# A gated attention layer on one core: the last attention unit's z and gate fill in pieces behind the logits of its second to sixth group, and the second gate weight split behind the sixth group's rows

## The chip, the core and the metric

The kernel runs on one core of a Trainium2 chip. The core has five engines with a queue of instructions each, worked off in order: TensorE (PE in the profile, its weight loads PEld), VectorE (DVE), ScalarE (ACT), GpSimd (POOL) and SyncE (SP), which here only issues transfers. Engines wait for each other by semaphores. TensorE writes into PSUM, which is divided into banks; the kernel keeps small pools of them. The metric is the time of one execution in microseconds (us), as the median of several runs.

## What is computed

One decoder layer for 1024 positions of 1024 channels, in float32. From the normed input one projection makes queries, keys, values, forget logits, z (the SiLU gates of the branches) and two gates per channel. Two attention branches follow: eight "fox" heads of 64 channels with a forget bias, and four "diff" heads with two maps each.

```python
h = rms_norm(x, g_pre[l], NORM_EPS)
proj = jnp.einsum('bsd,dn->bsn', h, w_in[l])
qa, ka, va, fa, za, qb, kb, vb, zb, gates = jnp.split(proj, SPLIT_POINTS, axis=-1)
ya = fox_attention(...)            # logits + c_t - c_s, causal softmax, times v
ya = merge_heads(ya) * jax.nn.silu(za)
yb = diff_attention(qd, kd, vd, lam)
yb = merge_heads(rms_norm(yb, g_subln[l], SUBLN_EPS) * (1.0 - lam_init)) * jax.nn.silu(zb)
gate_a, gate_b = jnp.split(jax.nn.sigmoid(gates), N_BRANCHES, axis=-1)
merged = gate_a * (ya @ w_branch[l, 0]) + gate_b * (yb @ w_branch[l, 1])
x = x + rms_norm(merged @ w_out[l], g_post[l], NORM_EPS)
```

## The kernel before

Every large product is made of three float32r products, high times high, high times low and low times high part; so each operand is split: a high part (a cast, mostly on ScalarE) and a low part (a subtraction, mostly on VectorE). A projection of 128 channels and 512 positions (`project`) is 24 matmuls of 512 columns: eight slices `k` of the 1024 input channels, three products each.

**Stages.** First the normed and transposed input `hT` and the values (lines to 297). Then eight attention units `u`: 0 to 3 are diff heads, 4 to 7 pairs of fox heads. Then the gates (first `pg`, a plain projection, then products by Winograd's scheme, `x_g`), the branch products `pb`, and the output product `x_o`.

**A fox unit** has eight groups: four pairs of query blocks `g` (in the last units in the order 3, 2, 1, 0), for each head `m` of the two. A group has two rows `i` (blocks of 128 queries). `s_row` makes a row: one or two pairs of matmuls put logits `Sf` into a PSUM bank (L487, L488; a pool of three banks); VectorE adds the bias `cb` and takes the minimum in one reduction (L490: writes `Pf`, `mxf`); ScalarE takes the exponential (L496, sum `lf`); VectorE the reciprocal (L617); GpSimd scales (L618). Ahead of each row GpSimd adds the mask to the diagonal of `cb` (L613). The `Pf` rows lie in a pool of six buffers, so a row's reduction waits until the transposes of the row six before it have been read. Then the group's `products` (`av`): TensorE transposes four blocks of 128 into a bank `ptf` (L517, two banks), ScalarE makes the high part `phf` (L520), VectorE the low part `plf` (L521), TensorE multiplies with the values (L541, `ypf`, one bank), and ScalarE and VectorE move the result out of that bank (`yt` L627, `ys` L628). The products of a group are issued after the rows of the next one.

**Fill.** Between the groups stand projections that attention does not wait for: queries and keys of the next unit, and `z` of a slice (`spill_tasks`: matmuls into a bank `pz`, a copy L428, a store L429). In unit 7 the fill list is z6 and z7, two halves of 24 matmuls each. `gate = spill_tasks("gl", ...)` makes the first gate's slice 0 the same way in two halves: `gate[0]` behind the logits of the sixth group (`GFILL = 5`), `gate[1]` in pieces among the last products, where an order is written out by `then` (`issue_after(lasts[0])`: what is issued inside is not placed before that instruction). The second gate's slice 0 is `gates_plain(0)`: `load_w` loads the weight and splits it, high part `hi_g` on ScalarE (L315), low part `lo_g` on GpSimd (L319); its matmuls `pg` come after the attention.

**What sets the order.** The program is recorded as it is written, and a scheduler with a model of times of its own (`schedule_with_timeline_sim=True`) then places each engine's instructions. So the matmuls of z stand where that scheduler put them, between other rows; only `issue_after` holds them back. Buffers of the weights are in pools of two (`wraw`, `whi`, `wlo`): `hi_g` takes the buffer of an earlier high part, and the load of the next gates' weight (`gate_raw`, `raw_1`) the buffer that `lo_g` has read.

Of the kernel before, what the change touches and what calls it, by code (L numbers as in the profile page):

```python
# [11 lines left out]
AF = mybir.ActivationFunctionType  # L12
# [19 lines left out]
YORD = ((), ((4, 0), (4, 1)), ((5, 0), (5, 1), (6, 0)), ((6, 1), (7, 0), (7, 1)),  # L32
        ((0, 0), (0, 1), (1, 0)), ((1, 1), (2, 0), (2, 1)), ((3, 0), (3, 1)), ())
GFILL = 5
TAIL = 3
ZFILL = ((0,), (1,), (), (2,), (3,), (4,), (5,), (6, 7))
BIG = 3.0e38
# [12 lines left out]
def tile_hybrid_block(  # L50
# [254 lines left out]
                h_combinations(k)  # L305


    def load_w(name, src, hi_act=False, lo_pool=False, pieces=None):
        raw = wpool.tile([P, KT, P], F32, tag="wraw", name=f"raw_{name}")
        for ks, piece in pieces or [(slice(0, KT), src)]:  # L310
            nc.sync.dma_start(raw[:, ks], piece)
        hi = wpool.tile([P, KT, P], F32R, tag="whi", name=f"hi_{name}")
        lo = wpool.tile([P, KT, P], F32R, tag="wlo", name=f"lo_{name}")
        if hi_act:
            nc.scalar.copy(hi, raw)  # L315
        else:
            nc.gpsimd.tensor_scalar(hi, raw, 1.0, 1.0, op0=ALU.mult, op1=ALU.mult)
        eng = nc.gpsimd if lo_pool else nc.vector
        eng.tensor_tensor(lo, raw, hi, op=ALU.subtract)  # L319
        return hi, lo  # L320

    def w_cols(c0):
# [12 lines left out]
    with ExitStack() as st:  # L335
# [140 lines left out]
        def s_row(T, m, i, X, bias, boff, nm, le=None):  # L476

            A, B = (T["TA"], T["KA"]) if m == 0 else (T["TB"], T["KB"])
            n = (i + 1) * P
            qs = slice(i * P, (i + 1) * P)  # L480
            xs = slice(i % 2 * P, (i % 2 + 1) * P)
            pr = pp.tile([P, S], F32, tag="P", name=f"P{nm}_{m}_{i}")
            mx = small.tile([P, 2], F32, tag="mx", name=f"mx{nm}_{m}_{i}", bufs=8)
            pcs = pieces(i)
            for j, (a, b) in enumerate(pcs):
                ps = sps.tile([P, CH], F32, tag="S", name=f"S{nm}_{m}_{i}_{j}")[:, 0:b - a]
                nc.tensor.matmul(ps, lhsT=A[:, qs], rhs=B[:, a:b], start=True, stop=False)  # L487
                lasts[0] = nc.tensor.matmul(  # L488
                    ps, lhsT=X[:, xs], rhs=B[:, a:b], start=False, stop=True).ins
                nc.vector.tensor_tensor_reduce(  # L490
                    out=pr[:, a:b], in0=ps, in1=bias[:, boff + a:boff + b], scale=-0.125,
                    scalar=BIG if j == 0 else mx[:, j - 1:j], op0=ALU.add, op1=ALU.min,
                    accum_out=mx[:, j:j + 1])
            if le is None:
                le = small.tile([P, 1], F32, tag="l", name=f"l{nm}_{m}_{i}", bufs=8)
            nc.scalar.activation(pr[:, 0:n], pr[:, 0:n], AF.Exp,  # L496
                                 bias=mx[:, len(pcs) - 1:len(pcs)], scale=-1.0, accum_out=le)
            return pr, le

        def av(rows, g, vt, hoff, fox, evac, nm, final):  # L500
# [55 lines left out]
        def unit_attn(u, T):  # L556
# [19 lines left out]
            if diff:  # L576
                def row(i, rows):
                    boff = S - (i + 1) * P
                    if "X" not in rows:
                        rows["X"] = [swapped(T, m, i // 2, f"d{u}") for m in range(2)]  # L580
                    le = small.tile([P, 2], F32, tag="l2", name=f"l{u}_{i}", bufs=4)
                    l1, l2 = le[:, 0:1], le[:, 1:2]
                    p1, _ = s_row(T, 0, i, rows["X"][0], dmask, boff, f"d{u}", l1)
                    p2, _ = s_row(T, 1, i, rows["X"][1], dmask, boff, f"d{u}", l2)
                    n = (i + 1) * P
                    nc.vector.reciprocal(le, le)
                    nc.gpsimd.tensor_scalar(
                        p2[:, 0:n], p2[:, 0:n], l2, nlam, op0=ALU.mult, op1=ALU.mult)
                    nc.scalar.activation(p1[:, 0:n], p1[:, 0:n], AF.Copy, scale=l1)
                    nc.gpsimd.tensor_tensor(  # L590
                        p1[:, 0:n], p1[:, 0:n], p2[:, 0:n], op=ALU.add)
                    rows[i] = p1

                def evac(g):
                    def run(yp):
                        ys = stg.tile([P, 2 * P], F32, tag="ys", name=f"ys{u}_{g}")
                        nc.scalar.copy(ys, yp)
                        nc.sync.dma_start(y_d[u][:, g * 2 * P:(g + 1) * 2 * P], ys)
                    return run

                for g in GORD[u]:
                    rows = {}
                    groups.append((
                        4 * g + 3,
                        [lambda i=i, rows=rows: row(i, rows) for i in (2 * g, 2 * g + 1)],
                        lambda g=g, rows=rows: av(rows, g, vt, 0, False, evac(g), f"d{u}_{g}", False)))
            else:
                ysb = {}

                def row(m, i, rows):  # L610
                    n = (i + 1) * P
                    diag = cb[m][:, n - P:n]
                    nc.gpsimd.tensor_tensor(diag, diag, trim, op=ALU.add)  # L613
                    if "X" not in rows:
                        rows["X"] = swapped(T, m, i // 2, f"f{u}")
                    p1, l1 = s_row(T, m, i, rows["X"], cb[m], 0, f"f{u}")
                    nc.vector.reciprocal(l1, l1)  # L617
                    nc.gpsimd.tensor_scalar(  # L618
                        p1[:, 0:n], p1[:, 0:n], l1, 1.0, op0=ALU.mult, op1=ALU.mult)
                    rows[i] = p1  # L620

                def evac(m, g):
                    def run(yp):
                        if m == 0:
                            ysb[g] = stg.tile([P, 2 * P], F32, tag="ys", name=f"ys{u}_{g}")
                        tmp = stg.tile([P, 2 * P], F32, tag="yt", name=f"yt{u}_{m}_{g}", bufs=1)
                        nc.scalar.copy(tmp[64:128], yp[64:128])  # L627
                        nc.vector.tensor_tensor(  # L628
                            ysb[g][64 * m:64 * m + 64], yp[0:64], tmp[64:128], op=ALU.add)
                        if m == 1:  # L630
                            nc.sync.dma_start(y_d[u][:, g * 2 * P:(g + 1) * 2 * P], ysb[g])
                    return run

                for g in GORD[u]:
                    for m in range(2):
                        rows = {}
                        groups.append((
                            4 * g + 3,
                            [lambda m=m, i=i, rows=rows: row(m, i, rows) for i in (2 * g + 1, 2 * g)],
                            lambda m=m, g=g, rows=rows: av(  # L640
                                rows, g, vt, m * P, True, evac(m, g), f"f{u}_{m}_{g}",
                                u == 7 and g in FING)))
# [40 lines left out]
        for u in range(8):  # L683
# [13 lines left out]
            for t in SFILL[u]:  # L697
                fill += [lambda t=t, c=c: sum_squares(t, c) for c in range(2)]
                fill.append(lambda t=t: subln_scales(t))
            total = sum(s[0] for s in groups)  # L700
            done, nf = 0, 0
            for n, (wgt, rws, prd) in enumerate(groups):
                if n == len(groups) // 2 and u < 7:
                    nxt = unit_attn(u + 1, T)
                    vload.append(nxt[1])
                for r in rws:
                    r()
                if pend and (u < 7 or n <= TAIL):
                    products(*pend())
                if u == 7 and n >= TAIL:  # L710
                    tail.append(prd)
                pend = prd
                done += wgt
                while nf < len(fill) and nf < len(fill) * done / total:
                    fill[nf]()
                    nf += 1
                if u == 7 and n == GFILL:
                    with tc.issue_after(lasts[0]):
                        gate[0]()
                    break  # L720

        def then(*fns):
            for f in fns:
# [152 lines left out]

    def gates_plain(d):
        for br in (1,):
            wt = load_w(f"g{br}_{d}", w_cols(GT + br * D + d * P), True, True)
            yield  # L880
            for c in range(2):
                ps = xps.tile([P, CH], F32, tag="x", name=f"pg{d}_{br}_{c}")
                project(ps, wt, c)
                gate_out(d, br, c, tmp.tile([P, CH], F32, tag="t", name=f"g{d}_{br}_{c}"), ps)
# [287 lines left out]
```

## Time and profile before

| | us |
|---|---|
| median of 3 runs | 903.33 |
| lowest, highest | 903.07, 904.46 |
| the profiled execution | 901.91 |
| its span, from the first instruction to the last | 900.1 |
| granted TensorE clock, mean | 0.998 |
| stage of the last unit's groups | about 530 to 583 |

The profile is of one execution. Its page gives busy time by engine, the chain of waits that ended last, and groups of instructions; the trace answers with windows, waits and rows in order of time. Instructions go by tile names without buffer numbers, out<-in. The unit's number is not in them: `Sf` and `ptf` near 530 are of unit 6 and 7. A matmul's row shows a modelled end that reaches into the next one; the distance between starts tells more.

| stretch of the trace | PE busy | DVE busy | ACT busy | POOL busy |
|---|---|---|---|---|
| 500 to 520 | 19.70 | 10.61 | 13.43 | 11.18 |
| 520 to 540 | 20.00 | 9.01 | 7.67 | 4.13 |
| 540 to 560 | 17.98 | 16.87 | 15.49 | 13.89 |
| 560 to 580 | 19.66 | 11.69 | 12.11 | 6.40 |
| 580 to 600 | 20.00 | 7.91 | 8.92 | 8.45 |

### The profile page before, as it was taken

Reading aid. Unit: us, or ns where it says so; the run is one execution under the profiler, and the core shown is the slowest. Engines: PE = TensorE matmul, PEld = TensorE weight load, DVE = VectorE, ACT = ScalarE, POOL = GpSimd, SP = SyncE. Lnnn points to the kernel's source line nnn. Section 1 sums busy time; section 2 is a strip of 40 time slices with the busy share of each in tenths; the row PEclk is TensorE's granted clock in tenths of the full one; section 3 lists DMA queues with packets and bytes.
Section 4 is the critical chain, followed back from the end, with each engine's and each line's share of the span. In section 5 each row is a group of like instructions: output and inputs, shape, how many; then the busy total and the mean of one; then the engine's idle time right before and its main releaser. Section 6 shows DMA issues by size and latency. Waiting matters only on the chain.

```text
span 900.1 us, 13797 instructions
## 1 busy us (share of the span) xinstructions
PE 883.0 (98%) x4600; PEld 745.7 (83%) x4600; DVE 577.5 (64%) x1122; ACT 428.8 (48%) x865; POOL 403.8 (45%) x398
## 2 busy tenths in 40 slices
PE   8999999999999999999999999999999999999996
PEld 6999987788888888888888887888888888888885
DVE  6766555767666644456547548525686896648796
ACT  7523224665756653464645537624453362314352
POOL 2134224735647535254444526415534223483961
PEclk9999999999999999999999999999999999999999
DMA  9566656756557763645636432197766598210495
GB/s 303 190 239 250 219 164 164 176 136 171 155 137 191 180 170 84 180 103 128 190 92 170 130 88 60 61 410 242 244 198 207 189 344 304 79 39 1 122 197 172
DMA packets 138185, 154.79 MB, mean 172 GB/s; under 512 B 12145, under 2 KB 98161, under 8 KB 137090
## 3 DMA queue, kind: packets, MB, share of 16 engines
q1 hardware_dynamic: 133744, 151.55, 56.0%
q0 software_dynamic: 4224, 2.10, 2.1%
q8 instruction: 36, 0.59, 0.3%
q14 instruction: 35, 0.29, 0.1%
q10 hardware_dynamic: 146, 0.27, 0.1%
HBM read 86.17 MB, written 38.34 MB: 138 GB/s over the span
## 4 chain that ended last, share of the span: by engine, by line
PE 82%; DMA 4%; DVE 4%; ACT 3%; SPq 2%; POOL 2%; issue 2%; POOLq 0%; DVEq 0%; ACTq 0%
PE x_g L812 15%; PE pb L972 10%; PE pv L213 10%; PE pz L329 9%; PE x_o L812 9%; PE pk L329 7%; PE pq L329 6%; PE ypf L541 3%; PE ptf L517 3%; PE ypd L541 2%; PE Sf L488 1%; SPq L361 1%; PE Sf L487 1%; PE pg L329 1%; DMA swk<-rawk 1%
## 5 line engine op out<-in xcount | busy, mean ns | idle before, releaser
L213 PE MATMUL pv<-wvhi,hT 128*128 128x264 f32 (+2 forms) x384 | 88.3, 324 | 0.6 <-ACT wvhi L159 0.6
L329 PE MATMUL pq<-hT,hi_q 128*128 128x512 f32 x256 | 82.1, 395 | 0.0
L329 PE MATMUL pz<-hT,hi_z 128*128 128x512 f32 x256 | 81.6, 394 | 0.2
L329 PE MATMUL pk<-hT,hi_k 128*128 128x512 f32 x256 | 81.7, 393 | 0.0
L972 PE MATMUL pb<-yT,hi_br 128*128 128x512 f32 x256 | 78.8, 389 | 0.0
L812 PE MATMUL x_g<-T,a_g 128*128 128x512 f32 x336 | 78.0, 391 | 0.0
L812 PE MATMUL x_o<-wo_op,a_o 128*128 128x512 f32 x336 | 77.6, 392 | 0.0
L812 PEld LDWEIGHTS x_o<-wo_op,a_o 128*128 128x128 f32 x336 | 63.0, 188 | 14.4 <-DVE a_o L762 0.5
L812 PEld LDWEIGHTS x_g<-T,a_g 128*128 128x128 f32 x336 | 63.1, 188 | 13.8
L213 PEld LDWEIGHTS pv<-wvhi,hT 128*128 128x128 f32 x384 | 64.4, 190 | 6.5 <-ACT wvhi L159 1.0
L496 ACT ACTIVATE Pd<-Pd,mxd 128x128 f32<-128x128 f32 (+7 forms) x64 | 49.7, 777 | 32.6 <-DVE mxd L490 32.5
L521 DVE TENSOR_TENSOR plf<-ptf,phf 128x512 fp32r<-128x512 f32 (+1 forms) x80 | 49.8, 635 | 21.5 <-ACT phf L520 20.9
L613 POOL TENSOR_TENSOR cb<-cb,trim 128x128 f32<-128x128 f32 x64 | 29.3, 462 | 76.2 <-DVE mxf L490 53.0
L213 PE MATMUL pv<-wvlo,hT 128*128 128x256 f32 (+2 forms) x192 | 61.7, 326 | 0.0
L496 ACT ACTIVATE Pf<-Pf,mxf 128x1024 f32<-128x1024 f32 (+3 forms) x64 | 49.7, 777 | 25.1 <-DVE mxf L490 24.8
L812 PE MATMUL x_g<-hT,a_g 128*128 128x512 f32 x252 | 59.1, 392 | 0.0
L618 POOL TENSOR_SCALAR Pf<-Pf,lf 128x1024 f32<-128x1024 f32 (+3 forms) x64 | 47.7, 750 | 21.7 <-DVE lf L617 19.2
L972 PEld LDWEIGHTS pb<-yT,hi_br 128*128 128x128 f32 x256 | 48.0, 188 | 9.9
L812 PEld LDWEIGHTS x_g<-hT,a_g 128*128 128x128 f32 x252 | 47.3, 188 | 10.4
L329 PEld LDWEIGHTS pz<-hT,hi_z 128*128 128x128 f32 x256 | 47.4, 188 | 9.5 <-DVE rotq L363 0.4
L329 PEld LDWEIGHTS pq<-hT,hi_q 128*128 128x128 f32 x256 | 47.2, 188 | 9.0
L329 PEld LDWEIGHTS pk<-hT,hi_k 128*128 128x128 f32 x256 | 47.0, 188 | 9.1 <-ACT sq L445 0.3
(262 smaller groups left out, 2271.8 us busy)
## 6 DMA issues: line engine op xcount, KB each, us to landing
t_d<-t SPq DMA_DIRECT2D x16, 512.0 KB, 4.2
T<-t_d SPq DMA_DIRECT2D x8, 1024.0 KB, 8.2
raw<-in_w_in_dram SPq DMA_DIRECT2D x14, 512.0 KB, 5.1
vb_d<-vbs SPq DMA_DIRECT2D x8, 512.0 KB
va_d<-vas SPq DMA_DIRECT2D x8, 512.0 KB, 3.8
raw_k<-in_w_in_dram SPq DMA_DIRECT2D x8, 512.0 KB, 4.6
raw_q<-in_w_in_dram SPq DMA_DIRECT2D x8, 512.0 KB, 4.9
V<-vb_d SPq DMA_DIRECT2D x4, 1024.0 KB, 6.4
```

Of the source, the lines that this page charges most:

```text
L213: nc.tensor.matmul(ps[n], lhsT=hT[hp][k // 4][i // 4][:, k % 4, hs], rhs=wt[k][:, a:b], start=first, stop=(k == KT - 1 and hp == 1))
L329: mm = nc.tensor.matmul(ps, lhsT=a[:, k, :], rhs=hT[h][k // 4][c][:, k % 4, :], start=(k == 0 and a is hi and h == 0), stop=(k == KT - 1 a ...
L361: nc.sync.dma_start(sw[b * 32:(b + 1) * 32, :], raw[o * 32:(o + 1) * 32, :])
L487: nc.tensor.matmul(ps, lhsT=A[:, qs], rhs=B[:, a:b], start=True, stop=False)
L496: nc.scalar.activation(pr[:, 0:n], pr[:, 0:n], AF.Exp, bias=mx[:, len(pcs) - 1:len(pcs)], scale=-1.0, accum_out=le)
L517: lasts[0] = nc.tensor.transpose(pt[:, o * P:(o + 1) * P], rows[2 * g + r][:, j * P:(j + 1) * P], ident).ins
L521: nc.vector.tensor_tensor(pl[:, 0:n], pt[:, 0:n], ph[:, 0:n], op=ALU.subtract)
L541: lasts[0] = nc.tensor.matmul(o, lhsT=a, rhs=b[:, src], start=(j == 0 and n == 0), stop=(odd == 1 and jj == g and n == len(prods) - 1)).ins
L613: nc.gpsimd.tensor_tensor(diag, diag, trim, op=ALU.add)
L618: nc.gpsimd.tensor_scalar(p1[:, 0:n], p1[:, 0:n], l1, 1.0, op0=ALU.mult, op1=ALU.mult)
L812: nc.tensor.matmul(x[m], lhsT=a[:, ai, k, :], rhs=right[m][bi][k], start=(k == 0 and n == 0), stop=(k == 3 and n == 2))
L972: nc.tensor.matmul(ps, lhsT=a[:, kk, :], rhs=yT[g][h][:, k % 2, sl], start=(k == 0 and a is hi and h == 0), stop=(k == 3 and a is lo))
```

## The change

Three edits, all in the last unit and the weight behind it.

1. The second half of z7 leaves the fill list and becomes `late[0]`; the first half of gl is `late[1]`. The table `LATE` gives, for each of the six first groups, which slices of which are issued behind the group's last logit matmul (`mark`): none in the first, slices 0 to 2 of z in the second, 3 to 5 in the third, 6 and 7 of z and 0 and 1 of gl in the fourth, 2 to 4 of gl in the fifth, 5 to 7 in the sixth. Each piece is held back by `issue_after(mark)`.
2. The rest of the fill of unit 7 (z6, first half of z7) is issued three times as early in the count of groups.
3. The high part of the second gate weight is held back behind the sixth group's last exponential (`held[0]`), its low part behind that group's last scaling (`held[1]`).

No arithmetic is added or taken away.

```diff
+LATE = ((), ((0, 0, 3),), ((0, 3, 6),), ((0, 6, 8), (1, 0, 2)), ((1, 2, 5),), ((1, 5, 8),))
...
-    def load_w(name, src, hi_act=False, lo_pool=False, pieces=None):
+    held = [None, None]
+
+    def load_w(name, src, hi_act=False, lo_pool=False, pieces=None, behind=(None, None)):
...
+        with tc.issue_after(behind[0]) if behind[0] else ExitStack():
+            if hi_act:
+                nc.scalar.copy(hi, raw)
...
+        with tc.issue_after(behind[1]) if behind[1] else ExitStack():
+            eng = nc.gpsimd if lo_pool else nc.vector
+            eng.tensor_tensor(lo, raw, hi, op=ALU.subtract)
...
+            late = [fill.pop(), gate[0]] if u == 7 else []
...
                 for r in rws:
                     r()
+                mark = lasts[0]
                 if pend and (u < 7 or n <= TAIL):
                     products(*pend())
...
-                while nf < len(fill) and nf < len(fill) * done / total:
+                while nf < len(fill) and nf < len(fill) * done * (3 if u == 7 else 1) / total:
                     fill[nf]()
                     nf += 1
-                if u == 7 and n == GFILL:
-                    with tc.issue_after(lasts[0]):
-                        gate[0]()
-                    break
+                if u == 7:
+                    for f, a, b in LATE[n]:
+                        with tc.issue_after(mark):
+                            late[f](range(a, b))
+                    if n == GFILL:
+                        behind = tuple(held)
+                        break
...
-            wt = load_w(f"g{br}_{d}", w_cols(GT + br * D + d * P), True, True)
+            wt = load_w(f"g{br}_{d}", w_cols(GT + br * D + d * P), True, True, behind=behind)
```

What the scheduler makes of it, at three places. In the names, `Sf_1_6_0` is unit 7's logits of head 1, row block 6, first piece; `ptf_0_2_2` the transposes of head 0, pair 2, third bank; the last number is a running one. Line numbers of the changed kernel are 5 higher here.

TensorE where unit 7's first rows begin, before (unit 6's last transposes and products around them):

```order
L517 MATMUL ptf_1_1_0_6128<-ident,Pf_1_3_6047 128x128
L487 MATMUL Sf_0_7_0_6209<-KA_5437,TA_5435 128x512
L488 MATMUL Sf_0_7_0_6209<-KA_5437,X0f_3_6204 128x512
L329 MATMUL pz_1_6628<-hT_91,lo_z_6496 128x512
L329 MATMUL pz_1_6628<-hT_91,hi_z_6495 128x512
```

and in the change, the piece of the second group, between its last logits and those of the third:

```order
L492 MATMUL Sf_1_6_1_6340<-KB_5438,TB_5436 128x384
L493 MATMUL Sf_1_6_1_6340<-KB_5438,X1f_3_6316 128x384
L334 MATMUL pz_1_6438<-hT_91,hi_z_6406 128x512
L334 MATMUL pz_1_6438<-hT_95,hi_z_6406 128x512
L334 MATMUL pz_1_6438<-hT_91,lo_z_6407 128x512
L334 MATMUL pz_1_6438<-hT_91,hi_z_6406 128x512
L334 MATMUL pz_1_6438<-hT_95,hi_z_6406 128x512
L334 MATMUL pz_1_6438<-hT_91,lo_z_6407 128x512
L334 MATMUL pz_1_6438<-hT_91,hi_z_6406 128x512
L334 MATMUL pz_1_6438<-hT_95,hi_z_6406 128x512
L334 MATMUL pz_1_6438<-hT_91,lo_z_6407 128x512
L492 MATMUL Sf_0_5_0_6454<-KA_5437,TA_5435 128x512
```

In the first listing z stands right behind unit 7's first logits (21 of its 24 matmuls are placed ahead of the second piece, `Sf_0_7_1`); in the change none stands before the second group's last logits, and nine do here. The others follow behind `Sf_0_4_1` (nine) and `Sf_1_4_1` (six, and six of gl).

VectorE behind the fifth group's rows, before:

```order
L617 RECIPROCAL lf_0_2_6624<-lf_0_2_6624 128x1
L628 TENSOR_TENSOR ys_3_6372<-ypf_1_3_6437,yt_1_3_6489 64x256
L490 ISA Pf_1_3_6660,mxf_1_3_6661<-Sf_1_3_0_6662,cb_1_6201 128x512
L490 ISA mxf_1_3_6661 128x1
L521 TENSOR_TENSOR plf_0_2_1_6572<-ptf_0_2_1_6570,phf_0_2_1_6571 128x512
```

and in the change:

```order
L622 RECIPROCAL lf_0_2_6665<-lf_0_2_6665 128x1
L495 ISA Pf_1_3_6682,mxf_1_3_6683<-Sf_1_3_0_6684,cb_1_6201 128x512
L495 ISA mxf_1_3_6683 128x1
L633 TENSOR_TENSOR ys_3_6400<-ypf_1_3_6481,yt_1_3_6533 64x256
L526 TENSOR_TENSOR plf_0_2_1_6591<-ptf_0_2_1_6589,phf_0_2_1_6590 128x512
```

The merge `ys_3`, which frees the one bank of products, has moved behind the reduction `Pf_1_3`.

ScalarE at the sixth group's exponentials, in the change; before, the cast `hi_g` (L315) stood ahead of unit 7's first exponential, and here `Pf_1_2` was followed by `phf_1_2_0`:

```order
L501 ACTIVATE Pf_1_3_6682,lf_1_3_6688<-Pf_1_3_6682,mxf_1_3_6683 128x512
L501 ACTIVATE Pf_1_2_6693,lf_1_2_6699<-Pf_1_2_6693,mxf_1_2_6694 128x384
L319 CAST hi_g_0_6956<-raw_g_0_6954 128x1024
L525 CAST phf_1_2_0_6719<-ptf_1_2_0_6718 128x512
L632 COPY yt_0_2_6619<-ypf_0_2_6579 64x256
L525 CAST phf_1_2_1_6728<-ptf_1_2_1_6727 128x512
```

The cast of 1024 columns has moved in between the sixth group's last exponential and the high parts of the fourth group's products (head 1, pair 2). On GpSimd `lo_g` follows the sixth group's last scaling, and on SyncE the load `raw_1` moves behind the stores of z, gl and `ys_3`.

More of the change, by code (lines that the diff above doesn't have):

```diff
@@ L313, in load_w @@
         lo = wpool.tile([P, KT, P], F32R, tag="wlo", name=f"lo_{name}")
[L314 to L319, printed above, removed]
+        with tc.issue_after(behind[0]) if behind[0] else ExitStack():
+            if hi_act:
+                nc.scalar.copy(hi, raw)
+            else:
+                nc.gpsimd.tensor_scalar(hi, raw, 1.0, 1.0, op0=ALU.mult, op1=ALU.mult)
+        with tc.issue_after(behind[1]) if behind[1] else ExitStack():
+            eng = nc.gpsimd if lo_pool else nc.vector
+            eng.tensor_tensor(lo, raw, hi, op=ALU.subtract)
         return hi, lo
@@ L495, in s_row @@
                 le = small.tile([P, 1], F32, tag="l", name=f"l{nm}_{m}_{i}", bufs=8)
-            nc.scalar.activation(pr[:, 0:n], pr[:, 0:n], AF.Exp,
-                                 bias=mx[:, len(pcs) - 1:len(pcs)], scale=-1.0, accum_out=le)
+            held[0] = nc.scalar.activation(pr[:, 0:n], pr[:, 0:n], AF.Exp,
+                                           bias=mx[:, len(pcs) - 1:len(pcs)], scale=-1.0, accum_out=le).ins
             return pr, le
@@ L617, in row @@
                     nc.vector.reciprocal(l1, l1)
-                    nc.gpsimd.tensor_scalar(
-                        p1[:, 0:n], p1[:, 0:n], l1, 1.0, op0=ALU.mult, op1=ALU.mult)
+                    held[1] = nc.gpsimd.tensor_scalar(
+                        p1[:, 0:n], p1[:, 0:n], l1, 1.0, op0=ALU.mult, op1=ALU.mult).ins
                     rows[i] = p1
```

## Prediction, made before the changed kernel was run

> **What bounds the kernel now.** I read the page first, then the busy time by windows around the change, then who waits for whom there, and last the rows in order of time.
>
> ```profile
> span 900.1 us, 13797 instructions
> PE 883.0 (98%) x4600; PEld 745.7 (83%) x4600; DVE 577.5 (64%) x1122; ACT 428.8 (48%) x865; POOL 403.8 (45%) x398
> PE 82%; DMA 4%; DVE 4%; ACT 3%; SPq 2%; POOL 2%; issue 2%; POOLq 0%; DVEq 0%; ACTq 0%
> ```
>
> TensorE (PE) bounds the whole: 98% busy and 82% of the chain of waits. The change neither adds nor removes a matmul, so it can only move PE's holes. The windows show where these lie (columns: us from the span's start, length, then busy time and count by engine, granted clock, DMA):
>
> ```profile
> 530.00:537.30 7.30, 7.30 (x43) 6.35 (x43) 2.45 (x9) 2.40 (x8) 1.77 (x4) 1.00 0.25 76
> 537.30:560.18 22.88, 20.86 (x131) 16.54 (x129) 19.32 (x59) 17.76 (x37) 13.89 (x18) 1.00 0.21 58
> 560.18:583.10 22.92, 22.58 (x147) 19.97 (x147) 13.28 (x40) 13.77 (x36) 9.03 (x16) 1.00 0.13 36
> ```
>
> Before 537 PE is full of z matmuls while VectorE (DVE) works a third of the time. From 537.3 to 560.2 it turns round: DVE 19.32 of 22.88 us, PE idle 2.02 us. From 560 PE is nearly full again, with the gl matmuls. A busy PE row hides short holes, since matmuls overlap. The waits of its weight loads (engine PEld) between 540 and 560 show more:
>
> ```profile
> PEld Sf L487 <- DVE mxf L490: 2.2, 7, 0.5
> PEld ypf L541 <- DVE plf L521: 1.3, 4, 0.4
> PEld ypf L541 <- DVE ys L628: 1.3, 3, 0.7
> PEld ypf L541 <- ACT phf L520: 0.9, 1, 0.9
> PEld ptf L517 <- DVE plf L521: 0.2, 1, 0.2
> ```
>
> That is 5.9 us, almost all for DVE: for the reduction that frees a bank for logits (mxf), for a low part (plf), for the merge that frees the product's bank (ys).
>
> **Part 1: z and gl pieces go into the holes.** The rows at the four largest holes, two for each (start, length, instruction; the idle time in brackets):
>
> ```profile
> 544.50 0.28 PE L488 MATMUL Sf<-KA,X0f 128*128 128x256 f32 x1
> 545.27 0.39 PE L541 MATMUL ypf<-phf,V 128*128 128x256 f32 x1 [0.48 <-DVE ys L628]
> ...
> 548.27 0.28 PE L488 MATMUL Sf<-KB,X1f 128*128 128x256 f32 x1
> 549.24 0.38 PE L541 MATMUL ypf<-phf,V 128*128 128x256 f32 x1 [0.69 <-ACT phf L520]
> ...
> 551.70 0.38 PE L541 MATMUL ypf<-phf,V 128*128 128x256 f32 x1
> 552.39 0.38 PE L487 MATMUL Sf<-KB,TB 128*128 128x256 f32 x1 [0.31 <-DVE mxf L490]
> ...
> 558.21 0.36 PE L541 MATMUL ypf<-phf,V 128*128 128x256 f32 x1
> 558.80 0.39 PE L541 MATMUL ypf<-plf,V 128*128 128x256 f32 x1 [0.23 <-DVE plf L521]
> ```
>
> To price them I need the distance of packed instructions, from the chain of waits, where they stand back to back:
>
> ```profile
> 532.52 3.65 PE pz L329 x16
> ...
> 566.94 1.05 PE ypf L541 x9
> 567.99 0.44 PE ptf L517 x4
> 568.43 0.29 PE ypf L541 x3
> 568.73 0.46 PE ptf L517 x4
> 569.19 1.39 PE pgl L329 x6
> ```
>
> A 512-column matmul takes 3.65/16 = 0.23 us, one of 256 columns 1.05/9 = 0.12, a transpose 0.44/4 = 0.11. From start to start the four places lose 0.77, 0.97, 0.69 and 0.59, less 0.12 each: 2.5 us. So the closed holes are worth at least the brackets, 1.7 us, and at most the weight loads' 5.9. Some of a load's wait lies under a running matmul, so I take the 2.5 that I counted and half of the other 3.4: **4.2 us**. The new pieces suffice: 24 z and 24 gl matmuls, 48 x 0.23 = 11 us, in blocks of 2 to 2.7 us between logits; and while PE does a block, DVE catches up. The stores of the two results move behind stores of y on SyncE, where nothing that PE reads is queued behind them but the load of part 3. The three-fold pace of the other fill moves no row of PE ahead of these.
>
> **Part 2: what the z matmuls covered.** They leave the stretch before 537, 21 of the 24 ahead of the three transposes of the previous unit that DVE's first reduction of unit 7 waits for (their read frees that row's buffer):
>
> ```profile
> 537.33 0.85 PE L517 MATMUL ptf<-ident,Pf 128*128 128x128 f32 x6
> ...
> 537.67 0.69 DVE L490 CUSTOM_DVE_ANT_0 Pf<-Sf,cb 128x512 f32<-128x512 f32 x1 [3.71 <-PE ptf L517]
> 538.40 0.42 DVE L628 TENSOR_TENSOR ys<-ypf,yt 64x256 f32<-64x256 f32 x1
> 538.85 0.56 DVE L521 TENSOR_TENSOR plf<-ptf,phf 128x384 fp32r<-128x384 f32 x1
> 539.32 0.74 DVE L490 CUSTOM_DVE_ANT_0 Pf<-Sf,cb,mxf 128x512 f32<-128x512 f32 x1
> ```
>
> So the row chain starts up to 21 x 0.23 = 4.8 us earlier, and DVE, idle for 3.71 us, can take it. This is what makes part 1 a gain: PE reaches the DVE-bound rows earlier and spends z there. Where is the new hole? The third logit pair of the second group (Sf_1_6_0) needs a bank that DVE's seventh instruction from there frees: four reductions, one merge, two low parts, 3 x 0.69 + 0.74 + 0.42 + 2 x 0.56 = 4.35, less about 0.07 of overlap at six of them: 3.9. PE has meanwhile, from the transposes' end, four logit pairs (3 x 0.46 + 0.35), eight products, two of them of 128 columns (0.82) and six transposes (0.66): 3.2. Hole: **0.7 us**. Its bounds are 0 and the 15 matmuls that are not given back before Sf_0_5_0, 3.4 us.
>
> **Part 3: two new waits in the sixth group's wake.** The rows of before, of three engines:
>
> ```profile
> 565.06 0.49 PE L517 MATMUL ptf<-ident,Pf 128*128 128x128 f32 x3
> ...
> 564.97 0.42 DVE L628 TENSOR_TENSOR ys<-ypf,yt 64x256 f32<-64x256 f32 x1 [3.43 <-ACT yt L627]
> 565.41 0.69 DVE L490 CUSTOM_DVE_ANT_0 Pf<-Sf,cb 128x512 f32<-128x512 f32 x1
> 566.03 1.15 DVE L521 TENSOR_TENSOR plf<-ptf,phf 128x512 fp32r<-128x512 f32 x2
> ...
> 569.14 0.69 DVE L521 TENSOR_TENSOR plf<-ptf,phf 128x512 fp32r<-128x512 f32 x1 [0.55 <-ACT phf L520]
> ...
> 539.14 1.05 ACT L315 CAST hi_g<-raw_g 128x1024 fp32r<-128x1024 f32 x1 [0.30 <-PE pz L329]
> ```
>
> First: DVE now has the merge ys_3 behind the reduction Pf_1_3, which waits for the three transposes at 565.06 (+0.35 us there). The products ypf_0_2 need ys_3 (one bank). From the first transpose: 0.35 + 0.61 + 0.42 + 0.05 = 1.43 us; PE has 0.33 of its own, and the six gl matmuls that stood there are gone. Hole: **1.1 us** (0 if DVE reaches ys_3 early, 1.4 at most).
>
> Second: the cast hi_g, 1.05 us on ScalarE (ACT), now stands between the exponential of Pf_1_2 and phf_1_2_0, ahead of phf_1_2_1. From the pair of low parts to the end of plf_1_2_0 before: 566.03 to 569.83, 3.80; with the cast 4.85. PE's rows in the chain from 566.94 to 570.58 are 3.64 before it needs that bank. Hole: 4.85 - 3.64, less 0.1 for the start: **1.1 us** (bounds 0 and 1.7, if phf_1_2_1 is caught too). What goes in return, the cast ahead of unit 7's first exponential, is part of the 4.2.
>
> The low part lo_g and a load behind it move too:
>
> ```profile
> 540.57 2.41 POOL L319 TENSOR_TENSOR lo_g<-raw_g,hi_g 128x1024 fp32r<-128x1024 f32 x1
> ...
> raw<-in_w_in_dram SPq DMA_DIRECT2D x14, 512.0 KB, 5.1
> ...
> 580.32 1.30 POOL L774 TENSOR_TENSOR S_g<-raw 128x512 f32<-128x512 f32 x1 [1.45 <-issue]
> ```
>
> The load of raw_1 waits for lo_g to free its buffer. In before's rows the cast would start some 0.6 us ahead of the low part at 569.14, where that one's high part starts, and end near 568.5 + 1.05 = 569.6 and lo_g near 572; loads of this kind land in 5.1 us by the page's median (its row in the middle), so by 577.1, and S_g reads it at 580.3. Behind this load on SyncE stand only two stores of y and the T loads of the next stage. Cost nothing; without those 3 us of cover, S_g would be late by as much as the load.
>
> **Sum**: -4.2 + 0.7 + 1.1 + 1.1 = **-1.3 us**. The profiled execution took 901.91 us (span 900.1 and 1.8 around it), so 900.6; the median of the runs is 1.42 above it, so the forecast is 903.33 - 1.3 = 902.0. About 0.2%, 1.8 us, is what a measurement can tell from no change.
>
> A rule that speaks against such moves: the window 537.30:560.18 has a granted clock of 1.00 although PE has holes of up to 0.85 us in it. The Trainium skill, "TensorE: Matmul & The Clock Gate", section "A second HAM failure mode: psum-queue depth-cycling", says that many short idles between matmul groups can make the clock fall back to half. By the trace the sum stays; by that rule the new hole stretch would cost what the fifth rival below says.
>
> **Rivals.**
> 1. Forecast, holes closed and half given back: -0.4 to -2.6, chance 0.55.
> 2. *The new waits do not bite*: DVE reaches ys_3 early, since it is ahead by part 2, and the cast falls into an idle stretch of ACT. Then -4.2 + 0.7 = -3.5: 899.8. For it: DVE sat idle for 3.43 us just ahead of that merge (its row above); against it: the reduction now stands between. Chance 0.16.
> 3. *Nothing but a move*: DVE and ACT set the pace from 531 to 560 whatever PE is given; the holes appear earlier by as much as they close. Closed 3.0, new 0.9 + 1.1 + 1.1: +0.1, so 903.4. DVE's 19.32 of 22.88 speaks for it, its 3.71 idle just before against. Chance 0.17.
> 4. *Slower, through GpSimd's queue*: the previous unit's last row is reduced only after a trim that stands behind one that waits for a transfer:
>
> ```profile
> 530.83 0.46 POOL L613 TENSOR_TENSOR cb<-cb,trim 128x128 f32<-128x128 f32 x1 [2.34 <-DMA cb<-cum_d]
> ```
>
> Before, z matmuls covered this wait. Now PE comes to a logit that needs that reduction near 532.9, and it can be done near 532.1: 0.8 us to spare. Each us beyond that is a us of PE; 3.9 us of delay would turn the sum to +1.8 and more: 905.1 to 906. Chance 0.10.
> 5. *The clock falls*: the 7.30 us of rows of the first window at half the rate cost 7 us more, 909. No window here shows under 1.00: chance 0.02.
>
> **How the numbers follow.** Faster by over 0.2% (under 901.5): the lower part of case 1 (0.21) and case 2: 0.37. Slower (over 905.1): case 4 and 5: 0.11. Same: the rest, 0.52. The range leaves out case 5, the outer half of 4 and the edge of 2: 899.9 to 904.8.
>
> **What would show it.** Right: the first reduction of unit 7 follows the transposes some 4 us earlier against the same row of PE, the weight loads' waits of 5.9 us fall under 2.5, and PE idles near 1 us ahead of ypf_0_2 and again ahead of the transposes that follow the cast, both by the name of DVE. Wrong: no PE hole behind the cast (case 2), over 2 us of holes in unit 7's first two groups (case 3), a trim's wait for cb<-cum_d on PE's chain (case 4). A change of PE's rows outside 530 to 583 would make the whole argument wrong.

## The result and the profile after

| | before | changed kernel |
|---|---|---|
| median, 22 runs each | 903.52 us | 901.90 us |
| lowest, highest | 901.92, 906.97 | 899.79, 905.04 |
| span of the profiled execution | 900.1 | 900.0 |

The ratio is 0.9983, 95% interval 0.9975 to 0.9990: 1.6 us less, with 0.9 to 2.3 inside the interval. The forecast was 902.0.

The two spans differ by 0.1 us only. So the first question is where the profiled execution lost the rest. Two rows bracket the changed stretch: a matmul of z that stands behind a group of transposes, with the same rows of PE up to it in both programs, and the first matmul of the second gate. Of the kernel before (start, length, then the instruction):

```profile
526.24 0.47 PE L329 MATMUL pz<-hT,lo_z 128*128 128x512 f32 x1
...
582.93 0.68 PE L329 MATMUL pg<-hT,hi_g 128*128 128x512 f32 x2
```

Of the changed kernel:

```profile
527.59 0.47 PE L334 MATMUL pz<-hT,lo_z 128*128 128x512 f32 x1
...
582.82 0.68 PE L334 MATMUL pg<-hT,hi_g 128*128 128x512 f32 x2
```

From row to row that is 56.69 us before and 55.23 now: **1.46 us less in the stage**. Ahead of it this execution was 1.35 us late, in rows of PE that both programs have alike; behind it, to the end of the span, both need 317.2. In the ten kernels of this study (the two programs and eight experiments) PE's rows up to the first of these two are the same, and it starts between 525.68 and 527.72. I take these 2 us as the scatter of one execution: the spans of the changed kernel's own 22 runs reach from 898.0 to 903.3. From here on I compare this **stage time**, not spans.

The windows of the changed kernel, in the columns of those before:

```profile
530.00:537.30 7.30, 7.30 (x53) 6.40 (x51) 5.51 (x18) 4.36 (x12) 1.73 (x4) 1.00 0.42 134
537.30:560.18 22.88, 22.41 (x137) 19.49 (x135) 15.62 (x48) 14.87 (x30) 11.22 (x16) 1.00 0.11 33
560.18:583.10 22.92, 21.05 (x139) 18.22 (x138) 14.41 (x43) 15.54 (x39) 12.02 (x18) 1.00 0.21 59
```

DVE's 19.32 us in the middle window have become 15.62, and 5.51 in the first in place of 2.45: the row chain starts earlier. PE's idle time in the middle went from 2.02 to 0.47 us; in the third window it rose from 0.34 to 1.87. So the gain was made in the middle and much of it was given back behind 560. How much these windows cannot say: a busy PE row hides short holes, and this execution stands 1.35 us later in them. The weight loads between 540 and 560 had waited 5.9 us; all that is left in that window is

```profile
PEld ypf L546 <- DVE plf L526: 0.3, 1, 0.3
```

What is left or new stands in these rows of PE:

```profile
537.63 0.40 PE L493 MATMUL Sf<-KB,X1f 128*128 128x512 f32 x1
538.37 0.50 PE L492 MATMUL Sf<-KB,TB 128*128 128x512 f32 x1 [0.34 <-DVE mxf L495]
...
563.39 0.95 PE L522 MATMUL ptf<-ident,Pf 128*128 128x128 f32 x7
565.36 0.39 PE L546 MATMUL ypf<-phf,V 128*128 128x256 f32 x1 [1.02 <-DVE ys L633]
...
569.00 0.40 PE L334 MATMUL pgl<-hT,lo_gl 128*128 128x512 f32 x1
569.91 0.55 PE L522 MATMUL ptf<-ident,Pf 128*128 128x128 f32 x3 [0.51 <-DVE plf L526]
```

I measure a hole as a **late start**: the distance from start to start, less the packed distances of the prediction (0.23 for a 512-column matmul, 0.12 for one of 256 columns, 0.11 for a transpose). These three places lose 0.51, 1.18 and 0.68 us: the third logit pair of the second group, the products ypf_0_2, and the transposes behind the cast. Smaller ones are 0.18 ahead of the row at 539.48 and 0.38 ahead of 549.81; 0.61 ahead of 578.17 was there before as well.

### The profile page after: what moved, and what is told of

Read it like the earlier page. It is cut to its first block, busy times and chain, and to the rows that moved or that the text cites. A ratio compares the mean times of both kernels' runs of the same rounds, so it can differ in the third digit from the quotient of the medians.

```text
span 900.0 us, 13801 instructions
## 1 busy us (share of the span) xinstructions
PE 882.5 (98%) x4600; PEld 745.7 (83%) x4600; DVE 579.8 (64%) x1122; ACT 429.2 (48%) x865; POOL 405.5 (45%) x398
## 4 chain that ended last, share of the span: by engine, by line
PE 77%; DMA 6%; DVE 5%; ACT 4%; SPq 3%; POOL 2%; issue 2%; POOLq 0%; DVEq 0%; ACTq 0%
PE x_g L822 15%; PE pb L982 10%; PE pv L214 10%; PE x_o L822 9%; PE pz L334 8%; PE pk L334 5%; PE pq L334 5%; PE ypf L546 3%; PE ptf L522 3%; SPq L366 2%; PE Sf L492 1%; PE ypd L546 1%; PE Sf L493 1%; DMA swk<-rawk 1%; PE pg L334 1%
## 5 line engine op out<-in xcount | busy, mean ns | idle before, releaser
L525 ACT CAST phf<-ptf 128x512 fp32r<-128x512 f32 (+1 forms) x80 | 42.4, 542 | 27.9 <-PE ptf L522 23.7
```

What stands on the lines that cost most here:

```text
L525: nc.scalar.copy(ph[:, 0:n], pt[:, 0:n])
```

## The experiments

**Theory A**: the stage is PE's work plus PE's holes, and each hole has a cause of its own that can be taken away alone. **Rival C**: DVE's and ACT's chain sets the pace of these rows, so that holes only move. **Rival B**: not the pieces made the gain, but the cast hi_g that left the first rows of unit 7.

### The wait on the cast taken out

```diff
-            wt = load_w(f"g{br}_{d}", w_cols(GT + br * D + d * P), True, True, behind=behind)
+            wt = load_w(f"g{br}_{d}", w_cols(GT + br * D + d * P), True, True)
```

> The changed kernel without the wait on the cast hi_g and the low part lo_g; PE's order is the same to the row. Theory A (the time is PE's work plus PE's holes, and each hole has its own cause): the hole of 0.68 us ahead of ptf_1_2_2 goes, the one of 1.18 us ahead of ypf_0_2 and that of 0.51 us ahead of Sf_1_6_0 stay, so some 0.8 us less than the changed kernel, about 2.4 us under the kernel before. Rival B (the cast had to leave the first rows of unit 7 for the gain): it comes back there and costs 1 us more than the changed kernel, 0.6 us under before. Rival C (DVE's work sets the pace, holes only move): the same as the changed kernel, 1.6 us under before.

Measured: 899.10 us against 901.96 of the kernel before on the same chip, ratio 0.9970 (0.9957 to 0.9982). The stage takes 54.21 us, 1.02 less than in the changed kernel. The hole ahead of ptf_1_2_2 is gone, those of 0.51, 0.38 and 1.18 are there to the hundredth. That is 0.68 of the 1.02; the rest, 0.34, are starts of under 0.12 us each that were late in the changed kernel in the transposes and products right behind that hole (569.9 to 571.3). So the wait **cost** a microsecond here, and nothing here speaks for rival B. It is not tested as it was put, since the cast did not go back to the first rows of the unit (the fourth experiment tests it): the scheduler now puts it between the two exponentials of the fourth group, where gl pieces stand on PE. The second row shows the longest wait of ACT in this stretch, 2.77 us, which a later run uses:

```profile
550.82 1.04 ACT L319 CAST hi_g<-raw_g 128x1024 fp32r<-128x1024 f32 x1
...
557.95 0.48 ACT L525 CAST phf<-ptf 128x384 fp32r<-128x384 f32 x1 [2.77 <-PE ptf L522]
```

### z in pieces, gl in one block

```diff
-LATE = ((), ((0, 0, 3),), ((0, 3, 6),), ((0, 6, 8), (1, 0, 2)), ((1, 2, 5),), ((1, 5, 8),))
+LATE = ((), ((0, 0, 3),), ((0, 3, 6),), ((0, 6, 8),), (), ((1, 0, 8),))
```

> The changed kernel with z in pieces, but all 24 gl matmuls in one block behind the logits of the sixth group, as before the change. Theory A: the pieces of z alone close the holes of 543 to 552; the merge ys_3 stands ahead of the reduction Pf_1_3 again and the hole of 1.18 us ahead of ypf_0_2 goes, while the 10 us between the fourth and the sixth group show only some 0.2 to 0.5 us of new holes: 0.5 to 0.9 us less than the changed kernel, 2.1 to 2.5 under before. My prediction's first part (gl pieces are needed in the holes of 552 to 559, which the start-to-start distances of before put at 1.5 us): 0.3 us slower or more than the changed kernel, 1.3 under before or less.

Measured: 899.75 us against 901.96, ratio 0.9975 (0.9964 to 0.9985). Stage 54.21 us, 1.02 less than the changed kernel. In the rows between 553 and 558, which the gl pieces were to fill, only 0.13 and 0.19 us of holes are left over; before, they summed to 1.51 between 552 and 559. With z behind the earlier groups, DVE is no longer late there. And on DVE the merge is back ahead of the reduction:

```profile
562.74 0.42 DVE L633 TENSOR_TENSOR ys<-ypf,yt 64x256 f32<-64x256 f32 x1 [3.73 <-ACT yt L632]
563.19 0.69 DVE L495 CUSTOM_DVE_ANT_0 Pf<-Sf,cb 128x512 f32<-128x512 f32 x1
```

so the hole ahead of ypf_0_2 is gone. The gl pieces were no help where they went, as long as the cast is held back.

### gl in pieces, z where it was

```diff
-LATE = ((), ((0, 0, 3),), ((0, 3, 6),), ((0, 6, 8), (1, 0, 2)), ((1, 2, 5),), ((1, 5, 8),))
+LATE = ((), (), (), ((1, 0, 2),), ((1, 2, 5),), ((1, 5, 8),))
...
-            late = [fill.pop(), gate[0]] if u == 7 else []
+            late = [None, gate[0]] if u == 7 else []
```

> The changed kernel with gl in pieces and the wait on the cast, but z's last 24 matmuls back in the fill ahead of unit 7. Theory A: the holes of the first groups of unit 7 stay (2 to 2.5 us), the new ones at ypf_0_2 and ptf_1_2_2 (1.9 us) come on top, and gl closes about 1.5: 0.2 to 0.8 us slower than the kernel before. Rival (the gl pieces are the gain): 1 us or more under before. Rival C (DVE sets the pace): within 0.3 us of before.

Measured: 904.28 us against 901.96, ratio 1.0027 (1.0016 to 1.0038), slower than before. The stage takes 57.24 us, 0.55 more than before: within what theory A said. The holes of 1.18 and 0.67 us opened, those of the first groups stayed (0.79, 0.51, 0.70 the largest). The other 1.8 us of the measured time are not in the stage. This profile loses 2.2 us between 127 and 157 us behind `pg`, most of it at 146, where the branch products wait for a split (the second row's bracket):

```profile
730.92 0.39 PE L982 MATMUL pb<-yT,hi_br 128*128 128x512 f32 x1
732.08 0.50 PE L982 MATMUL pb<-yT,hi_br 128*128 128x512 f32 x1 [0.78 <-DVE yT L972]
```

The changed kernel passes this place without a hole. I return to it below.

### The wait on the cast alone, in the kernel before

```diff
         with tc.issue_after(behind[0]) if behind[0] else ExitStack():
             if hi_act:
                 nc.scalar.copy(hi, raw)
...
+                    behind = tuple(held)
                     break
...
+            wt = load_w(f"g{br}_{d}", w_cols(GT + br * D + d * P), True, True, behind=behind)
```

> The kernel before with one edit of the change, the wait on hi_g and lo_g, which takes the cast from ACT's rows ahead of unit 7's first exponential to those behind the sixth group's. Theory A: the wait ahead of the transposes behind the cast opens (0.4 to 0.7 us), the rows at 539 to 545 lose about as much: within 0.3 us of before. Rival B (the cast was what delayed the first rows): 1 us under before.

Measured: 902.30 us against 901.96, ratio 0.9999 (0.9989 to 1.0009). Stage 56.42 us, 0.27 less than before. The edit by itself is worth next to nothing, as theory A said of the total. Of its terms the first came out small: the late start ahead of the transposes behind the cast is 0.19 us, not 0.4 to 0.7. Rival B, 1 us, falls. (This profile, too, has some 1.6 us more behind `pg`; the times do not show them.)

The four runs above make a small account of the stage: the wait alone -0.27; z in pieces on top of it -2.21 (56.42 to 54.21); gl in pieces on top of both **+1.02** (54.21 to 55.23). Sum -1.46. Taken in the other order, behind the wait, gl in pieces costs 0.82 (56.42 to 57.24) and z in pieces gains 2.01 (57.24 to 55.23). So the shares shift by some 0.2 with the order, and their signs do not.

### The last gl piece cut

The third slice of the last piece goes behind the transposes that the reduction Pf_1_3 waits for (`pmark` is the last transpose of the products recorded ahead of it):

```diff
+                    pmark = last_t[0]
...
-                        with tc.issue_after(mark):
+                        with tc.issue_after(pmark if a == 7 else mark):
...
-LATE = (..., ((1, 5, 8),))
+LATE = (..., ((1, 5, 7), (1, 7, 8)))
```

> The changed kernel with the last of gl's pieces cut: two slices behind the sixth group's logits as now, the third (three matmuls, 0.69 us) behind the transposes of ypf_0_2. The three transposes that the reduction Pf_1_3 waits for come earlier, and the copy of gl no longer stands ahead of yt on ACT, so ys_3 is merged ahead of that reduction. Theory A (ys_3 behind Pf_1_3 makes the hole of 1.18 us): the hole falls to 0.3 to 0.5 us, 0.6 to 0.8 us less than the changed kernel, 2.2 to 2.4 under before. Rival (DVE's own work up to ys_3 makes it): the 0.69 us of work are only moved ahead of the hole and it falls by as much as a new one ahead of plf_1_3_3 opens, 0.2 us or less.

Measured: 899.24 us against 901.99, ratio 0.9970 (0.9958 to 0.9982). Stage 54.16, 1.07 less than the changed kernel. PE's rows there are now

```profile
562.56 0.95 PE L522 MATMUL ptf<-ident,Pf 128*128 128x128 f32 x7
563.26 0.71 PE L334 MATMUL pgl<-hT,hi_gl 128*128 128x512 f32 x2
563.81 0.40 PE L334 MATMUL pgl<-hT,lo_gl 128*128 128x512 f32 x1
564.04 0.28 PE L547 MATMUL ypf<-phf,V 128*128 128x256 f32 x1
```

with no hole ahead of ypf_0_2; one of 0.34 stands at the sixth product, for a low part. The holes of over 0.12 us fell by 0.84 in all, a little above the 0.6 to 0.8 that I had written; the rest of the 1.07 are shorter late starts. On DVE the merge now stands ahead of the reduction:

```profile
563.16 0.42 DVE L634 TENSOR_TENSOR ys<-ypf,yt 64x256 f32<-64x256 f32 x1 [0.79 <-ACT yt L633]
563.61 0.69 DVE L495 CUSTOM_DVE_ANT_0 Pf<-Sf,cb 128x512 f32<-128x512 f32 x1
```

Two things were taken away together, the reduction ahead of the merge and the copy of gl ahead of yt; the run does not part them.

### A slice of z one group earlier

```diff
-LATE = ((), ((0, 0, 3),), ...
+LATE = (((0, 0, 1),), ((0, 1, 3),), ...
```

The pace of the other fill goes from three to five, so that z7's first half is recorded ahead of the slice.

> The changed kernel with the first slice of z's last half (three matmuls) one group earlier, behind the first group's logits. Theory A (part 2 of the prediction: Sf_1_6_0 waits for a bank since z was taken away from the rows ahead of it): the hole of 0.51 us there falls under 0.2 and nothing else opens, 0.4 to 0.6 us less than the changed kernel, about 2.1 under before. Rival (DVE sets the pace of these rows): the slice moves the hole behind itself, no change against the changed kernel.

Measured: 899.95 us against 901.99, ratio 0.9977 (0.9966 to 0.9989). Stage 54.72, 0.51 less than the changed kernel, as much as the hole that it aimed at. That hole is down to 0.09, from 0.51 (536.60 to 536.92, less 0.23):

```profile
536.60 0.40 PE L493 MATMUL Sf<-KB,X1f 128*128 128x512 f32 x1
536.92 0.50 PE L492 MATMUL Sf<-KB,TB 128*128 128x512 f32 x1
```

No hole over 0.12 us is left in the first two groups except one of 0.20. It is not so that nothing else opened: the holes of 0.18 and 0.38 us of the changed kernel are gone too, and beside the one of 0.20 there is a new one of 0.32 at 557.72, for a low part. These nearly cancel. Rival C, by which the time would have stayed, falls: DVE could follow.

### gl in one block and no wait

Both edits, of the first and of the second experiment.

> The changed kernel with gl in one block (as in z_late) and without the wait on the cast (as in no_hold). If the two gains of those runs add up: 1.7 to 2.0 us less than the changed kernel, 3.4 or more under before. If the cast, which the scheduler then puts between the two exponentials of the fourth group, was hidden in no_hold by the gl pieces that stand there: a new hole of about 1 us ahead of the products ypf_1_3, 0.7 us less than the changed kernel, 2.2 under before, as z_late.

Measured: 899.89 us against 901.99, ratio 0.9973 (0.9962 to 0.9983). Stage 54.25: no better than z_late's 54.21, as the second of the two expectations had it. The gains do not add, because the cast, at the same place on ACT as in the first experiment, has lost its cover:

```profile
551.39 1.04 ACT L319 CAST hi_g<-raw_g 128x1024 fp32r<-128x1024 f32 x1
552.33 0.57 ACT L433 COPY sz<-pz 128x512 f32<-128x512 f32 x1
552.80 0.83 ACT L501 ACTIVATE Pf<-Pf,mxf 128x640 f32<-128x640 f32 x1
553.54 0.19 ACT L501 ACTIVATION_READ_ACCUMULATOR Pf<-Pf,mxf 128x1 f32 x1
553.75 0.37 ACT L632 COPY yt<-ypf 64x256 f32<-64x256 f32 x1
```

The copy yt stands behind the cast, the merge behind yt, and PE waits for the merge:

```profile
553.33 0.40 PE L493 MATMUL Sf<-KB,X1f 128*128 128x512 f32 x1
554.62 0.39 PE L546 MATMUL ypf<-phf,V 128*128 128x256 f32 x1 [0.90 <-DVE ys L633]
```

From start to start that is 1.07 us of hole. So the cast does need a place; only the one that the change chose is not good. And theory A does not hold in its strict form: whether the cast makes a hole depends on what PE has to do meanwhile. Without the wait, gl in pieces costs nothing against one block (54.25 to 54.21), since the pieces cover the cast; with it they cost 1.02.

### A version made from the holes that are left

```diff
+LATE = (((0, 0, 2),), ((0, 2, 4),), ((0, 4, 6),), ((0, 6, 8),), (), ((1, 0, 8),))
...
+                cast = nc.scalar.copy(ph[:, 0:n], pt[:, 0:n]).ins
+                if (nm, jj) == ("f7_1_3", 2):
+                    held[0] = cast
...
-                        behind = tuple(held)
+                        behind = (held[0], None)
...
-        then(..., lambda: t5(1), piece(4, 5), ...)
+        then(..., lambda: t5(1), piece(4, 6), ...)
...
-        then(lambda: t6(0), lambda: t7(0), piece(5, KT), ...)
+        then(lambda: t6(0), lambda: t7(0), piece(6, KT), ...)
```

The pace of the other fill is five here too.

> A version made from the holes that are left: z's last half in four pieces of two slices, the first behind the first group's logits; gl's first half in one block behind the sixth group's; the cast hi_g held behind phf_1_3_2, where ACT is idle for 2.77 us in the changed kernel; in the tail two slices of gl in place of one ahead of ypf_1_1 (hole of 0.61 us, the same before and after the change). Theory A: the holes of 0.51, 0.38, 1.18, 0.68 and 0.61 us all go or nearly so, 3.5 to 4.2 us less than the changed kernel, 5 to 5.8 under before. Rival C (DVE sets the pace): 1.5 to 2.5 under before.

Measured: **895.96 us against 901.99, ratio 0.9936 (0.9920 to 0.9952)**, 6.0 us under the kernel before. Stage 51.08 us, 4.15 less than the changed kernel, at the upper end of what theory A said. PE is busy to the full in the windows that had holes:

```profile
530.00:537.30 7.30, 7.30 (x52) 6.57 (x50) 6.11 (x19) 4.94 (x12) 2.19 (x5) 1.00 0.34 98
537.30:560.18 22.88, 22.88 (x146) 20.39 (x145) 16.98 (x54) 17.35 (x36) 15.29 (x20) 1.00 0.18 50
560.18:583.10 22.92, 22.92 (x150) 20.58 (x150) 16.15 (x39) 16.07 (x37) 11.64 (x15) 1.00 0.34 115
```

The largest late start that is left in the stage is 0.12 us. Four things were changed at once here, so this run shows that the holes can all go, not what each edit is worth. The cast hides between two high parts for which ACT would wait anyway:

```profile
553.12 0.59 ACT L525 CAST phf<-ptf 128x512 fp32r<-128x512 f32 x1 [0.50 <-PE ptf L522]
553.60 1.05 ACT L319 CAST hi_g<-raw_g 128x1024 fp32r<-128x1024 f32 x1
554.55 0.48 ACT L525 CAST phf<-ptf 128x384 fp32r<-128x384 f32 x1
```

All runs together (stage and the rest of the span behind it from one profile each, in us):

| kernel | median | before, same chip | ratio (95%) | stage | behind it |
|---|---|---|---|---|---|
| before | - | 903.52 | 1 | 56.69 | 317.2 |
| changed | 901.90 | 903.52 | 0.9983 (0.9975-0.9990) | 55.23 | 317.2 |
| no_hold | 899.10 | 901.96 | 0.9970 (0.9957-0.9982) | 54.21 | 317.2 |
| z_late | 899.75 | 901.96 | 0.9975 (0.9964-0.9985) | 54.21 | 317.2 |
| gl_late | 904.28 | 901.96 | 1.0027 (1.0016-1.0038) | 57.24 | 319.4 |
| hold_only | 902.30 | 901.96 | 0.9999 (0.9989-1.0009) | 56.42 | 318.8 |
| split | 899.24 | 901.99 | 0.9970 (0.9958-0.9982) | 54.16 | 317.2 |
| z0 | 899.95 | 901.99 | 0.9977 (0.9966-0.9989) | 54.72 | 317.2 |
| zl_nh | 899.89 | 901.99 | 0.9973 (0.9962-0.9983) | 54.25 | 318.0 |
| best | 895.96 | 901.99 | 0.9936 (0.9920-0.9952) | 51.08 | 317.3 |

## Why the prediction was right, and where it was not

**The forecast and its sum.** -1.3 us were forecast; the stage gave -1.46, the times -1.6. Likeliest was "within 0.2%", and 0.17% with an interval of 0.10 to 0.25 lies at that bound. The terms came out as -4.0, +0.7 (two holes), +1.2 and +0.7, against -4.2, +0.7, +1.1 and +1.1. Put to the cast the 0.3 us of short late starts behind it, which no_hold takes away with its hole, and its term is +1.0 and the first -4.3. Either way no term is off by more than 0.4.

**Part 1, closed holes, 4.2 us.** The late starts of over 0.12 us between 543 and 559 summed to 3.78 before; 0.38 of them is left, and shorter ones fell from 3.56 to 2.92 in the stage. That is 3.78 - 0.38 + 0.64 = 4.0: the size is right. That is in part luck: the 2.5 us were counted from rows, but to take half of the other 3.4 us of the weight loads' waits was a guess, with no row for it. These waits overstate what PE loses: between 540 and 560 they fell from 5.9 to 0.3, over the whole stage (530 to 583) from 6.7 to 4.4, by 2.3 where the stage gained 1.46. **Wrong was whose work this is.** The prediction counted 24 z and 24 gl matmuls as what fills the holes. z alone did it: the holes of 552 to 559, 1.51 us before, went with work that stands ahead of them (z_late leaves 0.13 and 0.19 in the rows meant for gl). gl alone did not: in gl_late the first holes stay, and 0.70 and 0.32 of the later ones with them. I had read holes in a row as separate places to fill. I now read them as one cause, DVE being late since 543; no run shows that cause by itself.

**Part 2, Sf_1_6_0, 0.7 us.** Measured 0.51, and 0.18 two pairs further on. Cause shown by z0, which takes it away with three matmuls. DVE ran the seven instructions that the prediction lists, in that order, in 4.1 us (534.23 to 538.31), where 3.9 were reckoned. The start of the chain: the first reduction of unit 7 stands at 534.23 in place of 537.67, and this execution was 1.35 late, so 4.8 us earlier, the full 21 x 0.23.

```profile
534.23 0.69 DVE L495 CUSTOM_DVE_ANT_0 Pf<-Sf,cb 128x512 f32<-128x512 f32 x1
```

**Part 3, ypf_0_2, 1.1 us.** Measured 1.18, by the way that the prediction gave: the merge behind the reduction that waits for the transposes.

```profile
564.16 0.69 DVE L495 CUSTOM_DVE_ANT_0 Pf<-Sf,cb 128x512 f32<-128x512 f32 x1 [1.64 <-PE ptf L522]
...
564.89 0.42 DVE L633 TENSOR_TENSOR ys<-ypf,yt 64x256 f32<-64x256 f32 x1
```

Not seen was that the gl piece itself delays those transposes, and that its copy stands ahead of yt on ACT; split and z_late, two ways of changing this, both remove the hole.

**Part 3, the cast, 1.1 us.** Measured 0.68 for the hole, and 1.02 for the wait as a whole (no_hold): the mechanism holds, the hole was taken too large. From the pair of low parts to the end of plf_1_2_0 I took 4.85 us, the 3.80 of before and the whole cast; it was 4.51 (565.34 to 569.85). Part of the cast lies in a gap that ACT had there anyway. Before, the exponential ended at 568.31 and phf_1_2_0 started at 568.52, behind its transposes:

```profile
567.69 0.62 ACT L496 ACTIVATE Pf<-Pf,mxf 128x384 f32<-128x384 f32 x1
...
568.52 0.59 ACT L520 CAST phf<-ptf 128x512 fp32r<-128x512 f32 x1
```

In the changed kernel the cast starts where the exponential ends, and the next row starts 0.94 us later. Less the gap of 0.21, that is 0.73 us in place of 1.05, which gives about the 4.51:

```profile
567.00 0.62 ACT L501 ACTIVATE Pf<-Pf,mxf 128x384 f32<-128x384 f32 x1 [1.02 <-DVE mxf L495]
...
567.62 1.04 ACT L319 CAST hi_g<-raw_g 128x1024 fp32r<-128x1024 f32 x1
568.56 0.57 ACT L525 CAST phf<-ptf 128x512 fp32r<-128x512 f32 x1
569.16 0.37 ACT L632 COPY yt<-ypf 64x256 f32<-64x256 f32 x1
```

The load of raw_1 cost nothing, as said: the stretch behind `pg` is 317.2 us in both.

**The rivals.** The second (new waits do not bite) fell by both holes. The third (nothing but a move) fell by the middle window and by z0. The fourth, the trim behind the load of cb, came close as worked out: the trims ran at 532.16 to 533.04, the last reduction of unit 6 at 533.07 to 533.36, and PE came to the logit that needs it at 534.16, with the 0.8 us to spare that were reckoned. PE has no hole near it. The fifth did not occur: the clock is 1.00 in all three windows with the new holes of 0.5 to 1.2 us, so the rule of the Trainium skill, "TensorE: Matmul & The Clock Gate", section "A second HAM failure mode: psum-queue depth-cycling", did not bear here, as before the change.

**A sentence of the prediction that does not hold as it was put**: that a change of PE's rows outside 530 to 583 would make the argument wrong. Such a change is there, +1.35 us ahead of the stage, in rows that are the same in both programs, and within what one execution scatters.

**Left open**: why some of these kernels lose time at the branch products, 146 us behind the stage (0.8 us in the profile of zl_nh, 1.6 in hold_only, 2.2 in gl_late). In hold_only, the one I followed, SyncE's loads in the gate stage are issued in another order than before and some 50 us in 1.1 us later against `pg`, and the products later wait for the split yT. That the one causes the other is argued, not shown. No run took this alone, and the times show it in gl_late only.

## What to carry to other kernels

A row of holes on the bounding engine can have one cause at its start; here the later half of the row went with work placed ahead of it. Close the first ones, look again, and only then move more work, since each further piece also stands in front of something (here a gl piece delayed the transposes that a reduction, and behind it a merge, waited for). A long helper operation on an engine that works its queue in order may have a cheap place, a stretch in which that engine waits anyway (here 2.77 us, for a cast of 1.05). Look for it in the trace and hold the operation there: late it cost 0.7 to 1.0 us here, and where the scheduler put it 1.1, unless other work on PE covered it. For effects of this size compare two rows that bracket the stage, because the rest of one execution scatters by more than the effect.

## What was not expected of the hardware

Within the stage, equal rows repeat almost to the hundredth from one profile to the next: in three kernels that share the rows, changed, no_hold and split, the holes ahead of the second group's third logits, in the fourth group's products and in the tail measure 0.51, 0.38 and 0.61 us each time. Ahead of the stage, rows that are the same on PE start up to 2.04 us apart (525.68 to 527.72). Behind the stage seven of the ten need 317.2 to 317.3 us, and the other three lose 0.8 to 2.2 at the branch products. So a difference of 0.5 us in one stage could be read from one profile each, where the spans could not show it.
